# A two-layer hybrid block on one core: an instruction order planned with other durations, a fixed slack, the attention's second half ahead of a branch product, and 16-bit plane copies on ScalarE

## The chip, the cores and the metric

The kernel runs on 1 core of one Trainium2 chip. The metric is the device time of one execution in microseconds; lower is better. Engines are TensorE (PE; PEld is its weight load), VectorE (DVE), ScalarE (ACT), GpSimd (POOL) and SyncE (SP), which here issues nearly all DMAs.

## The reference

16 meta tokens and 256 input tokens (272 in all) of width 1024 go through two layers. A layer has a mixer of three branches and a feed-forward part:

```python
proj = rms_norm(h, g) @ w_in          # 12 parts: rq rk rv rg | hq hf hi hg | dq dk dv | mg
o_ret = retention(rq, rk, rv, rg)     # 4 heads, decayed causal attention, rms, * silu(gate)
o_hg  = hgrn2(hq, hf, hi, hg, lb)     # 8 heads, a gated recurrence with per-channel decay
o_da  = diff_attention(dq, dk, dv)    # 8 heads, softmax(.) - lam * softmax(.), times dv, rms
y = sum_n sigmoid(mg_n) * (branch_n @ w_branch[n])
h = h + y @ w_out
u = rms_norm(h, g2) @ w_ffn_in        # 5632 columns
c = conv_b + sum_j conv_w[j] * shift(u, j)      # 3 taps along tokens
h = h + (silu(gate half of c) * value half of c) @ w_ffn_out
```

A last rms_norm gives the output, 256 x 1024, in fp32.

## The kernel before, in words

Activations lie transposed: features on the 128 partitions, the 272 tokens along the free axis. The second layer computes 258 token columns where the earlier tokens' results are not needed (272 for keys, values and the recurrence's inputs).

**Large matmuls.** All weights come as one stream of 128 x 128 tiles, eight to a chunk of 512 KB. A chunk is fetched by SyncE (`wraw`, three buffers), ScalarE writes the rounded high part `whi`, VectorE the remainder `wlo` (four buffers each). The activations have high and low parts too (`xh` and `xl`, `b0hi` and `b0lo` and so on). A tile product is three matmuls, lines 915 to 917: `whi` by high, `whi` by low, `wlo` by high. Two column tiles of an output make a pair; a pair of a 1024-deep product is 16 tiles, 48 matmuls, and collects in one of two PSUM buffers named `main`. `products` issues it, `evacuate`, `rotate` (rotary embedding on VectorE) or a branch's own step reads it out.

**The list ORDER** names the pairs in the order in which TensorE takes them within a layer: `("b0", 2)` is the third pair of the first branch's product. Marks stand in between: `+name` traces the small work of a branch (`+hga`, `+hgb` the recurrence's two halves, `+hgoa`, `+hgob` their outputs, `+ret` retention, `+daa`, `+dab` the attention's two halves of four heads), `!name` sets the due time of that work, `*name` splits a branch's output into high and low parts. Small work means small fp32 matmuls on TensorE (tiles `lev`, `ho`, `ro`, `ds`, `wt`, `do`) linked to VectorE, ScalarE and GpSimd steps.

**The planner.** Nothing is issued while the program is traced. Every call becomes an operation with an engine, a cost in us (class `_Engine`), a key (the time on a clock made of the large matmuls' costs at which it is wanted), the tiles it touches, and what it depends on. `_Plan.order` then simulates the five engines: it takes again and again the operation that can start earliest, and among those that can start at the same moment the one with the lowest `rank`, mostly its key. A small matmul has its key plus HOLD (3.0), or minus PULL (8.0) where TensorE has just run another small matmul and its operands are SURE (0.3) old. BACK is charged for a return to large matmuls. A result is counted as seen by another engine CROSS (0.4) after its end. The order so found is written out; on the chip each engine takes its own queue in order and waits on semaphores. Costs are thus used to sort, never to delay.

`_Weights.next` gives a chunk's fetch and its two splits a key LEAD before the first tile's. `behind` traces a job of small work; within one kind a job's first operation is placed after the last operation of the job `apart` places before it. `settle` spreads the jobs' keys between the mark `+` and 12 us (MARGIN) before the mark `!`.

**Values.** v of each branch is needed with tokens on the partitions. `values` reads a pair out of PSUM into `vsrc` (ScalarE), and `to_tokens` turns it as 16-bit halves: two copies part the fp32 words into low and high planes (`apart`), SyncE issues two DMA transposes (`turned`), two more copies join the planes into `vt` or `rvt`. The copies were on GpSimd. There are 24 such pairs (hi, rv, dv: four each, in two layers). The three kinds of tile share four buffers.

GpSimd also does the sums over partitions for the norms of the heads (`hr`), small copies (`tails`, `dt`, `wts`), and eight multiplications by the row norm (`y`) where a norm is folded into the activations.

Of the kernel before, what the change touches and what calls it, by code (L numbers as in the profile page):

```python
# [39 lines left out]
SLOTS = 13  # L40
LEAD = 6.0
MARGIN = 12.0
# [5 lines left out]
HOLD, PULL = 3.0, 8.0  # L48
BACK = 0.09
SURE = 0.3  # L50


# [4 lines left out]
def _pairs(name, lo, hi):  # L57
# [18 lines left out]
    + [("+daa", 0), ("*b0", 0), ("!ret", 0), ("!hgob", 0)]  # L76
    + _pairs("dq", 2, 4) + _pairs("b0", 0, 4) + _pairs("dk", 2, 4) + _pairs("dv", 2, 4)
    + [("+dab", 0)]
    + _pairs("m1", 0, 4)
    + [("*b1", 0)]  # L80
# [276 lines left out]
class _Plan:  # L357
# [4 lines left out]
    FREE = 0.5  # L362
    SWITCH = 1.3
    SETS = {AF.Exp: "le", AF.Ln: "le", AF.Silu: "silu", AF.Sigmoid: "sigmoid"}

# [88 lines left out]
    def order(self):  # L454
# [15 lines left out]
        count = 0  # L470
        tables = "le"
        beside = False
# [22 lines left out]
        def rank(op, t):  # L495
            if op.engine == "pe" and op not in mains:
                return op.key - PULL if beside and op.fed + SURE <= t else op.key + HOLD
            late = 8.0 if op.func in self.SETS and self.SETS[op.func] != tables else 0.0
            return op.key + late
# [4 lines left out]
        while len(out) < todo:  # L504
# [69 lines left out]
class _Engine:  # L574
# [5 lines left out]
    def __getattr__(self, method):  # L580
        f = getattr(self.engine, method)

        def call(*args, **kw):
            aps = [(k, x) for k, x in list(enumerate(args)) + list(kw.items()) if isinstance(x, bass.AP)]
            outs = [x for k, x in aps if k in (0, "out", "accum_out")]
            ins = [x for k, x in aps if k not in (0, "out", "accum_out")]
            n = math.prod(outs[0].shape[1:])
            cost = self.fixed + self.each * n
            if self.name == "act":
                cost += 0.093 * (len(aps) - 2) - (0.043 if ins[0].tensor.name in self.plan.psum else 0.0)  # L590
            elif self.name == "pool" and method != "memset":
                cost += 1.6e-3 * n
            if method == "partition_all_reduce":
                cost = 0.4 + 5.4e-3 * n
            if method == "reciprocal":
                cost += 7 * self.each * n
            elif method == "tensor_tensor_scan":
                cost += self.each * n
            elif method == "transpose":
                cost = 0.11  # L600
            elif method == "matmul" and args[1].dtype == F32R:
                cost = max(0.107, n / 2400 + 0.003)
# [4 lines left out]
            self.plan.add(self.name, lambda: f(*args, **kw), cost, outs, ins, args[2] if method == "activation" else None)  # L607

        return call
# [57 lines left out]
def _trace(ctx, tc, plan, a, depth, probe):  # L667
    nc = tc.nc
    act = _Engine(plan, nc.scalar, "act", 0.094, 0.833e-3)
    dve = _Engine(plan, nc.vector, "dve", 0.068, 1.042e-3)  # L670
    pe = _Engine(plan, nc.tensor, "pe", 0.0, 4 / 2400)
# [220 lines left out]
    def products(xs, name, j, t0=0):  # L892
# [58 lines left out]
    def to_tokens(src, vt, e):  # L951
# [37 lines left out]
    for li in range(depth):  # L989
# [369 lines left out]

        def behind(f, until, apart=1):  # L1360


            plan.group = ops = []
            rest = f()
            plan.group = None
            plan.in_turn(ops)
            mine = chains.setdefault(until[:2], [])
            mine.append(ops)
            if len(mine) > apart:
                plan.queue(ops[0], mine[-1 - apart][-1])  # L1370
            jobs.append((until, clock[0], ops))
            return rest
# [24 lines left out]
        def final():  # L1397
# [15 lines left out]
            cost = 3 * (BANK / 2400 + 0.012)  # L1413
            groups = [(t, c) for t in range(2) for c in range(2)]
# [38 lines left out]
        for name, j in ORDER:  # L1453
# [9 lines left out]
            elif name in ("+daa", "+dab"):  # L1463
# [166 lines left out]
```

## Time and profile before

| | |
|---|---|
| median of 3 runs | 1304.77 us (1304.16 to 1307.01) |
| the profiled execution | 1305.7 us, span 1303.9 us |
| granted TensorE clock, mean | 0.998 |
| VectorE, ScalarE busy | 76%, 60% of the span |
| weight chunks fetched by SyncE | 402 of 512 KB and 4 of 256 KB |
| DMA transposes | 48, median 4.0 us from issue to landing |

The span runs from the first to the last instruction of the profiled execution; its time includes a little around it. In the profile, most of the program's instructions carry line 607 (before), where the helper that records every call issues them, so they are told apart by their tiles: `out<-in` after the engine and the operation. "Idle before, releaser" is the time in which an engine stood still before instructions of a group, and what ended most of it. A row of the windows view gives a stretch, then the busy time of PE, PEld, DVE, ACT and POOL in it with the count of instructions, the granted clock, the DMA engines' share and GB/s. A row of the waits view gives who waited for whom, the total in us, the number of times and the longest.

### The profile page before, as it was taken

What the parts mean: (1) busy time and instruction counts of PE and PEld (TensorE: products, weight loads), DVE (VectorE), ACT (ScalarE), POOL (GpSimd) and SP (SyncE); (2) the same over time, 40 slices, a digit from 0 to 9 for tenths busy, and PEclk for the clock granted to TensorE, in tenths of its full rate; (3) what the DMA queues carried; (4) which work ended last, traced back from release to release, by engine and by line L of the source; (5) the groups of instructions that cost most, each with busy time, mean ns of one, the idle gap of its engine ahead of it and who ended that gap; (6) DMA issues with size and microseconds to landing.
All of it is one profiled execution on the core that took longest, in us unless ns stands there. A gap on an engine that the chain in (4) does not pass through costs nothing.

```text
span 1303.9 us, 28637 instructions
## 1 busy us (share of the span) xinstructions
PE 1285.8 (99%) x11678; PEld 1256.7 (96%) x11678; DVE 986.7 (76%) x1589; ACT 786.7 (60%) x1282; POOL 270.3 (21%) x300
## 2 busy tenths in 40 slices
PE   9999999999999999999999999999999999999998
PEld 9999989999999999999999999899999999999986
DVE  7685897798686789886575768877986867898843
ACT  6746444746576567666456474447466765776643
POOL 5021262423422020000030212634223220200000
PEclk9999999999999999999999999999999999999999
DMA  7664665643744545555555646655446446466653
GB/s 272 200 179 147 173 178 155 164 160 125 199 138 157 182 156 178 183 173 183 175 178 185 186 149 185 179 155 168 159 138 199 145 162 198 144 207 196 201 190 112
DMA packets 86868, 225.36 MB, mean 173 GB/s; under 512 B 32976, under 2 KB 33104, under 8 KB 86736
## 3 DMA queue, kind: packets, MB, share of 16 engines
q1 hardware_dynamic: 86448, 223.00, 55.3%
q8 instruction: 92, 1.51, 0.5%
q10 hardware_dynamic: 288, 0.52, 0.1%
q14 instruction: 40, 0.33, 0.1%
HBM read 216.16 MB, written 1.05 MB: 167 GB/s over the span
## 4 chain that ended last, share of the span: by engine, by line
PE 88%; DVE 9%; issue 1%; ACT 1%; DMA 0%; SPq 0%; DVEq 0%; ACTq 0%
PE main L915 26%; PE main L917 26%; PE main L916 25%; DVE wlo L607 2%; PE fo L1430 2%; PE fo L1431 2%; PE fo L1429 2%; DVE two_b L607 1%; DVE two_a L607 1%; PE lev L1107 1%; PE ds L1291 1%; PE ho L607 1%; PE ro L607 1%; PE do L607 1%; DVE two_c L607 1%
## 5 line engine op out<-in xcount | busy, mean ns | idle before, releaser
L915 PE MATMUL main<-xh,whi 128*128 128x272 f32 (+1 forms) x2368 | 682.6, 288 | 0.8 <-ACT whi L607 0.8
L917 PE MATMUL main<-xh,wlo 128*128 128x272 f32 (+1 forms) x2368 | 673.9, 285 | 1.3 <-DVE wlo L607 0.7
L916 PE MATMUL main<-xl,whi 128*128 128x272 f32 (+1 forms) x2368 | 673.3, 284 | 1.5 <-DVE xl L607 1.5
L607 DVE TENSOR_TENSOR wlo<-wraw,whi 128x1024 fp32r<-128x1024 f32 (+1 forms) x411 | 512.0, 1250 | 187.8 <-ACT whi L607 186.6
L607 ACT ACTIVATE whi<-wraw 128x1024 fp32r<-128x1024 f32 (+1 forms) x411 | 427.5, 1042 | 250.9 <-PE main L916 166.3
L917 PEld LDWEIGHTS main<-xh,wlo 128*128 128x128 f32 x2368 | 446.5, 189 | 3.1 <-DVE wlo L607 2.3
L916 PEld LDWEIGHTS main<-xl,whi 128*128 128x128 f32 x2368 | 446.6, 189 | 2.2 <-DVE xl L607 1.9
L915 PEld LDWEIGHTS main<-xh,whi 128*128 128x128 f32 x2368 | 446.7, 189 | 2.0 <-ACT whi L607 1.0
L607 POOL TENSOR_TENSOR y<-h,rstd 128x272 f32<-128x272 f32 x32 | 34.6, 1112 | 318.1 <-ACT rstd L607 318.1
L607 POOL PARTITION_ALL_REDUCE hr<-hsq x36 | 65.8, 1837 | 88.9 <-ACT hsq L607 85.9
L607 DVE SCALAR_TENSOR_TENSOR two_b<-main,small,two_b 128x256 f32<-128x256 f32 (+2 forms) x144 | 65.3, 487 | 24.4 <-ACT two_b L607 22.7
L607 POOL COPY apart<-vsrc 128x512 uint16<-128x512 uint16 x48 | 40.7, 867 | 145.2 <-ACT vsrc L607 145.0
L607 ACT ACTIVATE two_b<-main,small 128x272 f32<-128x272 f32 (+1 forms) x72 | 37.3, 566 | 23.8 <-PE main L917 22.7
L915 PE MATMUL main<-ghi,whi 128*128 128x272 f32 x176 | 51.0, 290 | 0.0
L916 PE MATMUL main<-glo,whi 128*128 128x272 f32 x176 | 50.6, 287 | 0.0
L917 PE MATMUL main<-ghi,wlo 128*128 128x272 f32 x176 | 50.3, 286 | 0.0
L607 POOL COPY vt<-turned 128x512 uint16<-128x512 uint16 x32 | 37.0, 1160 | 29.2 <-DMA turned<-apart 29.0
L915 PE MATMUL main<-b0hi,whi 128*128 128x272 f32 (+1 forms) x128 | 37.9, 296 | 0.0
L915 PE MATMUL main<-b1hi,whi 128*128 128x272 f32 (+1 forms) x128 | 37.8, 296 | 0.0
L915 PE MATMUL main<-yhi,whi 128*128 128x272 f32 (+1 forms) x128 | 36.4, 284 | 0.0
L917 PE MATMUL main<-b0hi,wlo 128*128 128x272 f32 (+1 forms) x128 | 36.4, 284 | 0.0
L917 PE MATMUL main<-yhi,wlo 128*128 128x272 f32 (+1 forms) x128 | 36.3, 284 | 0.0
(235 smaller groups left out, 1970.1 us busy)
## 6 DMA issues: line engine op xcount, KB each, us to landing
wraw<-in_w SPq DMA_DIRECT2D x402, 512.0 KB, 3.4
h<-in_h SPq DMA_DIRECT2D x4, 272.0 KB, 5.1
dec<-in_dec SPq DMA_DIRECT2D x2, 544.0 KB, 4.9
wraw<-in_w SPq DMA_DIRECT2D x4, 256.0 KB, 4.2
const<-in_const SPq DMA_DIRECT2D x1, 937.0 KB, 5.6
turned<-apart SPq DMA_TRANSPOSE x48, 4.0
gain<-in_gl SPq DMA_DIRECT2D x1, 512.0 KB, 5.1
out<-y ACTq DMA_DIRECT2D x2, 256.0 KB, 2.8
```

Of the source, the lines that this page charges most:

```text
L607: self.plan.add(self.name, lambda: f(*args, **kw), cost, outs, ins, args[2] if method == "activation" else None)
L915: nc.tensor.matmul(o, wh, hi, start=first, stop=False)
L916: nc.tensor.matmul(o, wh, lo, start=False, stop=False)
L917: nc.tensor.matmul(o, wl, hi, start=False, stop=last)
L1107: nc.tensor.matmul(o, keys, x, start=True, stop=True)
L1291: nc.tensor.matmul(ss[m][:, at : at + nk], q[half, hd, q0 : q0 + P], k[half, hd, :nk], start=True, stop=True)
L1429: nc.tensor.matmul(o, gh, wh, start=False, stop=False)
L1430: nc.tensor.matmul(o, gl, wh, start=False, stop=False)
L1431: nc.tensor.matmul(o, gh, wl, start=False, stop=end)
```

## The change

Six things are changed; no operation is added or taken away.

- The costs that the planner gives to operations: fixed prices of ScalarE 0.094 to 0.2 and of VectorE 0.068 to 0.145 us, 0.01 instead of 0.003 us on each large matmul, own prices for GpSimd's copies, two-input operations and sums over partitions, 0.7 us more on a DMA transpose, and 8 us where GpSimd goes from two-input operations to sums over partitions or back.
- A small matmul whose operands are less than SAFE (1.0 us) old is ranked behind everything else. BACK becomes 0.
- LEAD goes from 6 to 8 us.
- In ORDER, the first branch's product b0 comes after dk and dv of the attention's second half and the mark `+dab`, not ahead of them.
- A head of the attention may start after the eighth operation from the end of the head two places before it, not after its last.
- The four plane copies of `to_tokens` are ScalarE activations (Copy), not GpSimd copies.

```diff
-LEAD = 6.0
+LEAD = 8.0
...
-BACK = 0.09
+BACK = 0.0
 SURE = 0.3
+SAFE = 1.0
...
-    + _pairs("dq", 2, 4) + _pairs("b0", 0, 4) + _pairs("dk", 2, 4) + _pairs("dv", 2, 4)
+    + _pairs("dq", 2, 4) + _pairs("dk", 2, 4) + _pairs("dv", 2, 4)
     + [("+dab", 0)]
-    + _pairs("m1", 0, 4)
+    + _pairs("b0", 0, 4) + _pairs("m1", 0, 4)
...
+    RELOAD = 8.0
...
             if op.engine == "pe" and op not in mains:
+                if op.fed + SAFE > t:
+                    return math.inf
                 return op.key - PULL if beside and op.fed + SURE <= t else op.key + HOLD
...
+            if e == "pool" and op.func is not None:
+                if op.func != code:
+                    code, t = op.func, max(t, engines[e] + self.RELOAD)
...
+            elif method == "tensor_scalar":
+                cost += 0.065 * (len(aps) - 2) - 0.14
+            elif method in ("scalar_tensor_tensor", "stream_shuffle", "tensor_tensor_reduce"):
+                cost += 0.06
...
+            elif self.name == "pool" and method == "tensor_tensor":
+                cost, kind = 0.55 + 2.1e-3 * n, method
+            elif self.name == "pool" and method == "tensor_copy":
+                cost = 0.5 + 1.6e-3 * n
+            elif method == "partition_all_reduce":
+                cost, kind = 0.2 + 6.3e-3 * n, method
...
-                cost = self.fixed + self.each * n * outs[0].shape[0]
+                cost = self.fixed + self.each * n * outs[0].shape[0] + (0.7 if kw.get("transpose") else 0.0)
...
-    act = _Engine(plan, nc.scalar, "act", 0.094, 0.833e-3)
-    dve = _Engine(plan, nc.vector, "dve", 0.068, 1.042e-3)
+    act = _Engine(plan, nc.scalar, "act", 0.2, 0.833e-3)
+    dve = _Engine(plan, nc.vector, "dve", 0.145, 1.052e-3)
...
-        cost = 3 * ((T - t0) / 2400 + 0.003)
+        cost = 3 * ((T - t0) / 2400 + 0.01)
...
-            pool.tensor_copy(apart[:, i].rearrange("p (c f x) -> p c f x", c=2, f=2),
-                             halves(src[:, :, : 2 * P], i).rearrange("p f (c x) -> p c f x", c=2))
+            act.activation(apart[:, i].rearrange("p (c f x) -> p c f x", c=2, f=2),
+                           halves(src[:, :, : 2 * P], i).rearrange("p f (c x) -> p c f x", c=2), AF.Copy)
...
-            pool.tensor_copy(halves(vt[:, :, e : e + 2 * P], i), turned[:, i].rearrange("p (c x) -> p c x", c=2))
+            act.activation(halves(vt[:, :, e : e + 2 * P], i), turned[:, i].rearrange("p (c x) -> p c x", c=2), AF.Copy)
...
-        def behind(f, until, apart=1):
+        def behind(f, until, apart=1, after=1):
...
-            mine.append(ops)
+            mine.append((ops, after))
             if len(mine) > apart:
-                plan.queue(ops[0], mine[-1 - apart][-1])
+                before, which = mine[-1 - apart]
+                plan.queue(ops[0], before[-which])
...
-                    behind(lambda: da_head(b, hd), "da", 2)
+                    behind(lambda: da_head(b, hd), "da", 2, 8)
```

More of the change, by code (lines that the diff above doesn't have):

```diff
@@ L470, in order @@
         count = 0
-        tables = "le"
+        tables, code = "le", "tensor_tensor"
         beside = False
@@ L588, in call @@
             cost = self.fixed + self.each * n
+            kind = args[2] if method == "activation" else None
             if self.name == "act":
                 cost += 0.093 * (len(aps) - 2) - (0.043 if ins[0].tensor.name in self.plan.psum else 0.0)
[L591 to L595, printed above, removed]
-                cost += 7 * self.each * n
-            elif method == "tensor_tensor_scan":
-                cost += self.each * n
+            elif method == "tensor_scalar":
+                cost += 0.065 * (len(aps) - 2) - 0.14
+            elif method in ("scalar_tensor_tensor", "stream_shuffle", "tensor_tensor_reduce"):
+                cost += 0.06
+            elif method == "reciprocal":
+                cost += 7 * self.each * n
+            elif self.name == "pool" and method == "tensor_tensor":
[4 more added lines that the diff above has]
+                cost, kind = 0.2 + 6.3e-3 * n, method
             elif method == "transpose":
                 cost = 0.11
-            elif method == "matmul" and args[1].dtype == F32R:
-                cost = max(0.107, n / 2400 + 0.003)
             elif method == "matmul":
@@ L605, in call @@
             elif method == "dma_start":
-                cost = self.fixed + self.each * n * outs[0].shape[0]
-            self.plan.add(self.name, lambda: f(*args, **kw), cost, outs, ins, args[2] if method == "activation" else None)
+                cost = self.fixed + self.each * n * outs[0].shape[0] + (0.7 if kw.get("transpose") else 0.0)
+            self.plan.add(self.name, lambda: f(*args, **kw), cost, outs, ins, kind)
         return call
@@ L1412, in final @@
                     pe.matmul(accs[t][k // 4][:, k % 4 * P : (k % 4 + 1) * P], h[:, k, tokens(t)], ident, is_transpose=True, start=k % 4 == 0, stop=False)
-            cost = 3 * (BANK / 2400 + 0.012)
+            cost = 3 * (BANK / 2400 + 0.0133)
             groups = [(t, c) for t in range(2) for c in range(2)]
```

## The prediction

> **What bounds the kernel now.** I read the page's busy table first, then TensorE's own waits, then the stages in which those waits lie, then what GpSimd does there.
>
> ```profile
> span 1303.9 us, 28637 instructions
> ## 1 busy us (share of the span) xinstructions
> PE 1285.8 (99%) x11678; PEld 1256.7 (96%) x11678; DVE 986.7 (76%) x1589; ACT 786.7 (60%) x1282; POOL 270.3 (21%) x300
> ```
>
> TensorE is busy for 1285.8 of 1303.9 us, and the change removes no matmul. So what can be won by order alone is TensorE's idle time, 18.1 us at most, and whatever its instructions lose inside their busy time. The list of who TensorE waited for, longest first, says where the idle time is:
>
> ```profile
> PE lev L1107 <- DVE hf L607: 3.2, 2, 1.7
> PE main L916 <- DVE xl L607: 1.5, 2, 1.1
> PE ho L607 <- DVE ho L607: 1.4, 2, 0.8
> PE wt L1317 <- DVE two_a L607: 1.1, 3, 0.5
> PE warm L607 <- POOL eps L607: 1.0, 1, 1.0
> PE main L915 <- ACT whi L607: 0.8, 1, 0.8
> PE main L917 <- DVE wlo L607: 0.7, 3, 0.3
> PE lev L1107 <- DVE tot L607: 0.4, 1, 0.4
> PE lev L1107 <- DVE hq L607: 0.4, 1, 0.4
> PE main L917 <- issue: 0.4, 1, 0.4
> PE do L607 <- DVE tw L607: 0.4, 1, 0.4
> ```
>
> These eleven rows hold 11.3 us (total, times, longest). Two kinds stand in it. Small matmuls of the chains (lev of the HGRN2 levels, ho of its outputs, wt and do of the attention) were put into TensorE's queue before VectorE had their operands: 3.2 + 0.4 + 0.4 = 4.0 us for lev, 1.4 + 1.1 + 0.4 = 2.9 us for ho, wt and do. And the large ones waited at the start and at the feed-forward's first tiles, 1.5 + 1.0 + 0.8 + 0.7 + 0.4 = 4.4 us. VectorE ends nearly all of it. So I looked at the two stages with lev of the second half (155 to 206 and 806 to 860 us), at the stages of dv's first half, and at the stretch after the longest wait:
>
> ```profile
> 155.00:206.00 51.00, 48.83 (x761) 47.34 (x760) 45.28 (x70) 25.44 (x44) 31.19 (x33) 1.00 0.77 187
> 243.00:266.00 23.00, 22.19 (x181) 22.01 (x180) 18.22 (x21) 15.92 (x26) 16.12 (x17) 1.00 0.64 161
> 806.00:860.00 54.00, 51.86 (x781) 50.44 (x779) 45.53 (x70) 25.58 (x44) 32.30 (x34) 0.97 0.71 178
> 895.00:920.00 25.00, 24.43 (x199) 24.23 (x198) 19.59 (x27) 16.70 (x28) 16.09 (x17) 1.00 0.59 166
> ...
> 834.00:836.00 2.00, 2.00 (x10) 2.00 (x10) 2.00 (x4) 1.43 (x3) 0.06 (x1) 0.50 0.52 135
> 836.00:838.00 2.00, 2.00 (x65) 1.85 (x67) 0.59 (x1) 0.00 (x0) 0.00 (x0) 0.71 0.79 211
> ```
>
> The columns are PE, PEld, DVE, ACT, POOL busy, then granted clock. Three things are to be seen. In the lev stage VectorE works 45.28 of 51 us and ScalarE only 25.44, so the engine that ends the waits is nearly full, and another is half empty. GpSimd, elsewhere at 21% of the span, works 31.19 us there. And in the second layer TensorE's clock falls: 0.50 from 834 to 836 and 0.71 from 836 to 838, which is 2 x 0.50 + 2 x 0.29 = 1.6 us of full-speed work lost right after lev's 1.7 us wait.
>
> **The 16-bit planes.** The groups of the stage 155 to 206 us show why VectorE is slow there:
>
> ```profile
> L607 DVE TENSOR_TENSOR wlo<-wraw,whi 128x1024 fp32r<-128x1024 f32 x14 | 19.1, 1370 | 3.0 <-ACT whi L607 2.8
> L607 ACT ACTIVATE whi<-wraw 128x1024 fp32r<-128x1024 f32 x14 | 14.8, 1056 | 7.3 <-PE main L916 6.3 <-ACT at L607 1.0
> L607 POOL COPY apart<-vsrc 128x512 uint16<-128x512 uint16 x12 | 9.8, 839 | 20.7 <-ACT vsrc L607 20.6
> L607 POOL COPY rvt<-turned 128x512 uint16<-128x512 uint16 x8 | 7.2, 924 | 12.6 <-DMA turned<-apart 12.6
> L607 POOL COPY vt<-turned 128x512 uint16<-128x512 uint16 x4 | 5.4, 1340 | 2.4 <-DMA turned<-apart 2.2
> ...
> L607 ACT ACTIVATE vsrc<-main 128x544 f32<-128x544 f32 x6 | 3.7, 623 | 4.7 <-PE main L917 4.5 <-issue 0.3
> ```
>
> wlo takes 1370 ns on average in this stage; its median over the whole run, by the view of that tile, is 1224:
>
> ```profile
> L607 DVE TENSOR_TENSOR wlo<-wraw,whi x411: 418/1224/2232, 6.0 to 1288.0; 128x1024 fp32r<-128x1024 f32 x132, 128x512 fp32r<-128x512 f32 x4, 128x256 fp32r<-128x256 f32 x1
> ```
>
> That is 12% more while GpSimd copies. If the rest of VectorE's work there is stretched alike, 45.28 x (1 - 1224/1370) = 4.8 us of the 45.28 come back when the copies leave GpSimd; I take that as the upper end, for some of GpSimd's work stays, and 0 as the lower.
>
> The copies now cost ScalarE. No row shows it on 16-bit elements. The nearest is vsrc, 544 elements in 623 ns, so 512 cost about 0.62 us; the far end is GpSimd's own time:
>
> ```profile
> L607 POOL COPY apart<-vsrc 128x512 uint16<-128x512 uint16 x48 | 40.7, 867 | 145.2 <-ACT vsrc L607 145.0
> L607 POOL COPY vt<-turned 128x512 uint16<-128x512 uint16 x32 | 37.0, 1160 | 29.2 <-DMA turned<-apart 29.0
> ...
> L607 POOL COPY rvt<-turned 128x512 uint16<-128x512 uint16 x16 | 15.7, 1011 | 27.7 <-DMA turned<-apart 27.7
> ```
>
> So 48 + 32 + 16 = 96 copies move; GpSimd loses 40.7 + 37.0 + 15.7 = 93.4 us and ScalarE gains 96 x 0.62 = 60 (93 at the far end). I take 0.62, since whi, also ScalarE's, keeps 1056 ns in the very stage where wlo is stretched. In 155 to 206 us ScalarE goes from 25.44 to 25.44 + 24 x 0.62 = 40.3 of 51; in 243 to 266 from 15.92 to 20.9 of 23. On its average it fits. What is new is the wait: a joining copy waits for its transposing DMA, and what stands behind it in ScalarE's queue is whi of the weights to come, then wlo on VectorE, then the large matmuls. The cover is this row of the waits over all engines:
>
> ```profile
> ACT whi L607 <- PE main L916: 166.3, 134, 2.9
> ```
>
> 134 times ScalarE stood ready and waited for a whi buffer, so mostly it is ahead by all four. I charge 0.7 us for the planes, with 0 and 12.2 (worked out under the rivals) as ends.
>
> **The true durations and the slack.** The planner priced a large tile at 3 x (272/2400 + 0.003) = 0.349 us, and a chunk's wlo at 0.068 + 1024 x 0.001042 = 1.135 us. Before, wlo took 1.224, and VectorE's shorter instructions, which carry the larger fixed price now, were under-priced by more. So small matmuls were queued for a moment at which VectorE was not ready. That is the first kind of wait: 4.0 us of lev, 2.9 of the others, and the 1.6 us of clock. With the true prices and 1.0 us of slack (SAFE) a small matmul is ranked behind the large ones until its operands are 1 us old in the plan. What hides that delay are large matmuls, which are nearly always ready. What is late next is then the chain itself, and its jobs are spread over tens of microseconds. I let 80% of it go, as VectorE stays near full in the lev stage: (4.0 + 1.6) x 0.8 = 4.5 and 2.9 x 0.8 = 2.3 us.
>
> [...]
>
> The price of the slack is that runs of small matmuls may break into more pieces. Each return to large ones costs something inside TensorE's busy time:
>
> ```profile
> 135.09 0.38 PE L915 MATMUL main<-xh,whi 128*128 128x272 f32 x1
> 135.31 0.29 PE L916 MATMUL main<-xl,whi 128*128 128x272 f32 x1
> 135.44 0.28 PE L917 MATMUL main<-xh,wlo 128*128 128x272 f32 x1
> ```
>
> From the timeline of TensorE, just after an ho run: the first large matmul holds the next back by 0.22 us, the second by 0.13. A return costs 0.09. BACK leaves the plan, but nothing on the chip changes by that. Between 10 returns fewer and 16 more (one for each of the 2 x 8 attention heads) the end is -0.9 to +1.5; I take +0.5.
>
> **LEAD of 8.** Weights are fetched and split 2 us earlier in the plan. At the feed-forward's first tiles (xl, wlo: 1.5 + 0.7) this helps; I take 0.8 of the 4.4 us of the second kind, bounds 0 and 2.2. At the very start it moves the second chunk's DMA ahead of the second pair of h tiles: its key goes from 3 - 6 = -3 to 3 - 8 = -5, and that pair has 1.4 x 2 - 7 = -4.2. The first 30 us move
>
> ```profile
> DMA packets 3025, 8.49 MB, mean 283 GB/s; under 512 B 464, under 2 KB 592, under 8 KB 3024
> ```
>
> so 512 KB in front of those tiles cost 0 to 1.85 us; I take 0.7, as both are needed by the same matmuls.
>
> **The second half first.** b0's four pairs (DMA stream, 192 large matmuls, four VectorE products) go behind dk and dv of the second half, so its attention may begin four pairs, about 24 us, earlier (48 matmuls of 0.125 us a pair), and b0's operand slots are held that much longer. The heads have more room up to the same due time; wt and do above are what this can save, so I charge it with nothing further, between -1 and +1.5 us (their waits gone, or as much again). The DMA's 0.7 us, the 8 us that the plan now charges GpSimd for a change of its code and the other prices act only through order: nothing more.
>
> Sum: -4.5 - 2.3 - 0.8 + 0.7 + 0.5 + 0.7 = -5.7 us. The profiled execution took 1305.7 us (span 1303.9); that gives 1300.0. The median of the three runs, 1304.77, lies 0.9 below the profiled one, so the forecast is 1299.1 us. With every term at its kind end (-5.6, -2.9, -2.2, 0, -0.9, 0 and -1 for the order) it is 1292.2; with -4.5, -2.3, 0, +1.85, +1.5 and +0.7 it is 1302.
>
> **Rivals.** *ScalarE's queue stalls behind the transposes (slower).* In the rows above GpSimd waited 12.6 + 2.2 = 14.8 us for them in 155 to 206 us, 29.0 + 27.7 = 56.7 in all. If ScalarE sits through the same, it needs 40.3 + 14.8 = 55.1 of 51 us, 4.1 too many, and the like in the second layer; with 56.7/48 = 1.2 us for each of four joins, 243 to 266 needs 20.9 + 4.7 = 25.6 of 23, and 895 to 920 16.7 + 5.0 + 4.7 = 26.4 of 25. Together 4.1 x 2 + 2.6 + 1.4 = 12.2 us. It decides once a join waits over (51 - 40.3)/12 = 0.9 us on average in the first stage. With this price whole, and the other terms (-6.4) kept, the profiled sum is 1311.5 and the time 1310.6. For it: the transposes share SyncE's queue with the weights. Against: GpSimd had nothing better to do while it waited, and 134 waits for whi buffers are cover. Chance 0.24.
>
> *The waits only move (no change).* VectorE's 45.28 of 51 us stay a deficit, since it gets back little of the 4.8; a small matmul that comes later is then still too early, or its chain pushes a later one. With half of 4.5 + 2.3 gone and the start, returns and planes at their worse middles (1.0 + 1.0 + 1.0), the sum is -3.4 - 0.4 + 3.0 = -0.8: 1304.0. Chance 0.13.
>
> *The clock drops all the same.* If the half-clock stretch hangs on something other than the wait, or returns at another gap, 1.3 of the 4.5 us stay: 1300.4. Chance 0.06. [...]
>
> **How the numbers follow.** The forecast has 0.57, and its own range is 1292 to 1302. About 0.2% (2.6 us) is what a measurement of this kernel can tell from no change. Faster: 0.57 + 0.06, less 0.01 that ends within the bound, 0.62; same 0.14; slower 0.24. The range that leaves out no more than 2 in 10 runs from the kind end, 1292, to just above the slower rival, 1311.
>
> **What the changed profile would show.** Right: lev's waits for VectorE under 1 us in sum, no window under clock 0.9 near 830 us, wlo near 1.25 us in the values' stages, POOL near 177 us busy and ACT near 847, the 96 copies near 0.62 us. Wrong: ScalarE's joining copies waiting for the transposes by more than 0.9 us each with main matmuls waiting for whi or wlo behind them; copies near 1 us; a second-layer clock still at 0.50; or main waiting at 6 to 14 us for xl of the h tiles by over 1 us more.

## The result, and the profile after

| | before | after |
|---|---|---|
| median beside each other | 1305.67 us | 1301.59 us |
| ratio, with its 95% interval | | 0.9977 [0.9968, 0.9986] |
| the profiled execution | 1305.7 us, span 1303.9 | 1303.02 us, span 1301.2 |

The change makes the kernel faster by 0.23%, 3.0 us (1.8 to 4.2). The forecast was 5.7 us: the sign is right and the size about half. The busy table of the changed kernel answers to the one of before:

```profile
span 1301.2 us, 28596 instructions
## 1 busy us (share of the span) xinstructions
PE 1285.1 (99%) x11678; PEld 1257.0 (97%) x11678; DVE 960.2 (74%) x1589; ACT 831.8 (64%) x1374; POOL 167.7 (13%) x204
```

The copies moved as they should: GpSimd has 102.6 us less, ScalarE 45.1 more, and VectorE, which has the same 1589 instructions, works 26.5 us less. (ScalarE's groups by themselves add up to 58.9 us more, 896.7 against 837.8; time in which two of its instructions overlap in the trace counts once in the busy table.) TensorE's own waits in the changed kernel, the whole list (total, times, longest):

```profile
PE main L926 <- DVE xl L617: 5.8, 6, 1.9
PE main L927 <- DVE wlo L617: 2.0, 4, 0.7
PE warm L617 <- POOL eps L617: 1.0, 1, 1.0
PE main L925 <- DVE dq L617: 0.8, 1, 0.8
PE main L925 <- DVE dk L617: 0.2, 1, 0.2
PE main L925 <- ACT xh L617: 0.2, 1, 0.2
```

Every wait of a small matmul is gone: 4.0 us of lev and 2.9 of ho, wt and do. In their place stand waits of the large ones: for xl 5.8 instead of 1.5 us, for wlo 2.0 instead of 0.7, for the rotation of dq (it holds the PSUM buffer) 0.8. The windows of the stages shown before, and of a stretch that is new (PE, PEld, DVE, ACT, POOL, then granted clock):

```profile
155.00:206.00 51.00, 51.00 (x773) 49.69 (x775) 38.85 (x65) 38.76 (x68) 5.17 (x9) 1.00 0.84 198
243.00:266.00 23.00, 23.00 (x186) 22.84 (x185) 15.33 (x25) 20.99 (x32) 4.46 (x9) 1.00 0.55 161
806.00:860.00 54.00, 54.00 (x813) 52.73 (x812) 42.92 (x72) 39.80 (x71) 4.41 (x10) 1.00 0.81 198
895.00:920.00 25.00, 25.00 (x205) 24.89 (x204) 20.92 (x37) 20.80 (x37) 10.56 (x11) 1.00 0.53 167
...
834.00:836.00 2.00, 2.00 (x75) 1.83 (x74) 0.58 (x2) 1.46 (x2) 0.21 (x1) 1.00 0.41 80
...
1131.00:1133.00 2.00, 1.23 (x5) 1.23 (x6) 2.00 (x6) 2.00 (x5) 0.00 (x0) 0.66 0.57 217
1133.00:1135.00 2.00, 2.00 (x11) 2.00 (x11) 2.00 (x4) 0.48 (x2) 0.00 (x0) 0.50 0.00 0
```

TensorE is now busy in all of the four stages, VectorE has fallen from 45.28 to 38.85 us in the first, and the clock at 834 us is full. It is 0.66 and 0.50 at 1131 to 1135 instead: 2 x 0.34 + 2 x 0.50 = 1.7 us lost there.

Where the time came from and went is read from TensorE's timeline, by the start of the first large matmul of a pair (us; the pair's place follows from ORDER and 48 matmuls a pair):

```
                                           before +   after, copies   after, old   last kernel
first matmul of           before   after   copies     on GpSimd       prices       below
layer 1  hf 3              37.6     42.1     37.6        40.3           38.9         37.2
         rv 0             161.4    165.2    161.4       163.4          162.1        160.4
         dq 0             193.0    192.8    191.1       192.3          189.9        187.9
         first ffn pair   466.9    466.9    464.9       465.0          463.8        461.2
layer 2  rv 0             814.2    814.6    812.3       813.5          811.5        808.6
         dq 0             847.1    842.2    840.0       840.2          839.0        835.3
         first ffn pair  1110.1   1105.6   1103.6      1106.4         1102.2       1100.5
span                     1303.9   1301.2   1297.4      1300.8         1296.6       1295.6
```

The changed kernel loses 4.5 us before hf 3, wins 4.0 and 5.3 us in the two lev stages (rv 0 to dq 0), and gives 1.8 back after 1110. Elsewhere it differs by under 1 us. Both half clocks are in these numbers: about 1.7 of the 5.3 us is the one that the profiled execution of before had at 834, and the 1.8 us after 1110 are nearly all the one at 1131.

### The profile page after: what moved, and what is told of

Same layout as the page of the kernel before. It is cut to its first block, busy times and chain, and to the rows that moved or that the text cites. A ratio compares the mean times of both kernels' runs of the same rounds, so it can differ in the third digit from the quotient of the medians.

```text
span 1301.2 us, 28596 instructions
## 1 busy us (share of the span) xinstructions
PE 1285.1 (99%) x11678; PEld 1257.0 (97%) x11678; DVE 960.2 (74%) x1589; ACT 831.8 (64%) x1374; POOL 167.7 (13%) x204
## 4 chain that ended last, share of the span: by engine, by line
PE 92%; DVE 6%; issue 1%; DMA 1%; ACT 0%; SPq 0%; DVEq 0%
PE main L925 27%; PE main L926 27%; PE main L927 27%; DVE wlo L617 2%; PE fo L1442 2%; PE fo L1441 2%; PE fo L1440 2%; PE lev L1117 1%; DVE two_b L617 1%; PE ds L1301 1%; PE ro L617 1%; PE do L617 1%; DMA wraw<-in_w 1%; PE ho L617 1%; DVE xl L617 1%
## 5 line engine op out<-in xcount | busy, mean ns | idle before, releaser
L617 DVE TENSOR_TENSOR wlo<-wraw,whi 128x1024 fp32r<-128x1024 f32 (+1 forms) x411 | 505.1, 1236 | 179.3 <-ACT whi L617 178.6
L617 POOL PARTITION_ALL_REDUCE hr<-hsq x36 | 74.2, 2077 | 128.1 <-ACT hsq L617 127.9
L617 ACT ACTIVATE two_b<-main,small 128x272 f32<-128x272 f32 (+1 forms) x72 | 37.7, 566 | 26.7 <-PE main L927 26.7
L617 ACT ACTIVATE m<-main 128x544 f32<-128x544 f32 (+1 forms) x24 | 14.7, 614 | 39.5 <-PE main L927 39.5
L927 PE MATMUL main<-b1hi,wlo 128*128 128x272 f32 (+1 forms) x128 | 36.5, 285 | 0.5 <-DVE wlo L617 0.5
L926 PE MATMUL main<-b1lo,whi 128*128 128x272 f32 (+1 forms) x128 | 36.4, 284 | 0.0
```

What stands on the lines that cost most here:

```text
L926: nc.tensor.matmul(o, wh, lo, start=False, stop=False)
L927: nc.tensor.matmul(o, wl, hi, start=False, stop=last)
```

## The experiments

The gain in us is (1 - ratio) x 1305. The interval is the ratio's, at 95%.

| kernel | ratio | interval | gain, us |
|---|---|---|---|
| the change | 0.9977 | 0.9968 - 0.9986 | 3.0 |
| before + copies on ScalarE | 0.9961 | 0.9946 - 0.9975 | 5.1 |
| the same, ScalarE's price nudged | 0.9964 | 0.9951 - 0.9978 | 4.7 |
| the same, VectorE's price nudged | 0.9955 | 0.9941 - 0.9968 | 5.9 |
| before + copies + slack | 0.9969 | 0.9956 - 0.9981 | 4.0 |
| before + copies + all new prices | 1.0050 | 1.0038 - 1.0063 | -6.5 |
| ... only ScalarE's and VectorE's | 1.0018 | 1.0009 - 1.0028 | -2.3 |
| ... only the large matmuls' | 0.9986 | 0.9977 - 0.9994 | 1.8 |
| ... only GpSimd's, with the 8 us | 1.0015 | 1.0006 - 1.0025 | -2.0 |
| ... only GpSimd's, without them | 0.9984 | 0.9974 - 0.9993 | 2.1 |
| before + LEAD 8 | 1.0023 | 1.0014 - 1.0032 | -3.0 |
| the change, copies on GpSimd | 0.9987 | 0.9978 - 0.9995 | 1.7 |
| the change, no slack | 1.0017 | 1.0008 - 1.0026 | -2.2 |
| the change, LEAD 6 | 0.9996 | 0.9987 - 1.0005 | 0.5 |
| the change, b0 first again | 0.9992 | 0.9983 - 1.0002 | 1.0 |
| the change, old prices | 0.9953 | 0.9941 - 0.9965 | 6.1 |
| the change, h fetched first | 0.9978 | 0.9969 - 0.9987 | 2.9 |
| the change, start repaired | 0.9967 | 0.9956 - 0.9979 | 4.3 |
| the last kernel below | 0.9941 | 0.9928 - 0.9953 | 7.7 |

My first theory was that the change is what I had forecast, less a start that was put in disorder. The rival: the planner's part is worth little or less than nothing, and the copies carry the gain.

**The copies alone.** Before, with the copies on ScalarE and nothing else:

```diff
-            pool.tensor_copy(apart[:, i]...
+            act.activation(apart[:, i]..., AF.Copy)
...
-            pool.tensor_copy(halves(vt...
+            act.activation(halves(vt..., AF.Copy)
```

> The kernel before with the plane copies on ScalarE alone, old prices and order rules. If the copies' going frees VectorE where lev waits (forecast): wlo near 1.22 us in 155 to 206 us, lev's waits fall from 4.0 us, time 1302 to 1304. If what counts is the plan's prices and slack: within 1 us of 1305.7 or slower, with lev, ho and wt still waiting about 7 us. If ScalarE's queue stalls behind the transposes: slower by over 3 us, with main waiting for whi or wlo.

It gains 5.1 us, more than the 1302 to 1304 us expected of it and, by the middle values, more than the whole change (the intervals overlap in a small part). Its list of TensorE's waits, whole:

```profile
PE main L916 <- DVE xl L607: 1.5, 2, 1.2
PE wt L607 <- DVE wts L607: 1.5, 2, 1.1
PE wt L1317 <- DVE two_a L607: 1.3, 3, 0.5
PE warm L607 <- POOL eps L607: 1.0, 1, 1.0
PE main L917 <- DVE wlo L607: 0.5, 2, 0.3
PE lev L1107 <- issue: 0.4, 1, 0.4
```

lev no longer waits for VectorE and neither does ho, with the old prices and no slack; the attention's wt does, and the start is as it was (hf 3 at 37.6). Its windows of the lev stages:

```profile
155.00:206.00 51.00, 50.57 (x777) 49.17 (x776) 40.97 (x72) 40.21 (x69) 5.57 (x9) 1.00 0.77 197
806.00:860.00 54.00, 54.00 (x810) 52.62 (x809) 42.78 (x78) 41.36 (x72) 6.36 (x10) 1.00 0.74 192
```

VectorE is busy 4.3 us less in the first, close to the 4.8 that I had worked out and left out of the sum, and over the whole run 25.6 us less with the same 1589 instructions (986.7 to 961.1).

**LEAD of 8 on the kernel before** (`LEAD = 6.0` to `8.0`):

> The kernel before with LEAD 8 alone. T1: 4 us slower at the start, as the fetch order there becomes that of the changed kernel, up to 1 us won back elsewhere: 1308 to 1310. T2: no change, 1305 to 1306. T3: slower by the two feed-forward starts, about 2 us, 1307 to 1308, with the start unchanged.

3.0 us slower. The fourth fetch of h goes out at 8.18 instead of 4.96 us, hf 3 begins at 39.4 instead of 37.6, and the large matmuls wait 4.1 us for xl. So LEAD 8 does harm at the start by itself, 1.8 us; the other 1.2 us are lost later.

**LEAD of 6 in the changed kernel** (`LEAD = 8.0` to `6.0`):

> The changed kernel with LEAD back at 6. Theory T1 (the loss sits in SyncE's queue at the start: with LEAD 8 the fourth chunk's fetch, which waits for a wraw buffer, stands ahead of the last pair of h tiles): the fourth h fetch is issued near 5 us instead of 8.55, rstd is ready near 21.5 us instead of 26.3, the pair hf 3 starts near 37.6 us instead of 42.1, and the time falls by about 4.5 us, to 1297. Rival T2 (true durations, not LEAD, delay the folded activations on GpSimd and VectorE): the start stays as in the changed kernel and the time stays within 1 us of 1301.6. T3 (LEAD 8 costs mostly at the two feed-forward starts, by putting wlo ahead of xl on VectorE): the waits of 1.5 us near 492 and 2.2 us near 1129 us go, the start stays, 1298.

It loses 2.5 us against the change, though h is fetched as before: the start stays late (hf 3 at 42.3), and the large matmuls wait 3.9 us for wlo, eight times. My first theory expected 1297 us and is refuted: LEAD is not what holds up the start of the changed kernel. With the new prices the longer lead pays; in the kernel before it does not.

**The start.** First the fetches of h moved ahead, then also the squares of the norm, and the slack kept away from the first norm's matmul:

```diff
 # both
-plan.key = -9.0 if k == 0 else 1.4 * k - 7.0
+plan.key = -9.0 if k == 0 else 1.4 * k - 9.0
 # the second alone
-                plan.key = 1.0 + 2.5 * j
+                plan.key = -1.5 + 2.5 * j
...
-                if op.fed + SAFE > t:
+                if op.key > 30.0 and op.fed + SAFE > t:
```

> The changed kernel with LEAD 8 kept and the keys of the h fetches put 2 us earlier, so that SyncE issues them in the order of the kernel before; nearly all the rest of the order stays. T1: the start as in the kernel before (hf 3 near 37.6 us), 4 to 4.5 us less, 1297 to 1297.6. T2 and T3: no change, 1301 to 1302.

> The changed kernel with three things at the start alone: the h fetches' keys 2 us earlier (as in e2_h_first), the four squares of the first norm 2.5 us earlier, and no slack for the first norm's matmul. T4 (the start lost 4.5 us to late rstd, by three causes in one chain: SyncE's order, the squares behind whi on ScalarE, and the slack on the norm's matmul): rstd done near 21.5 us, hf 3 near 37.6 to 38 us, time 1297 to 1298. T5 (the start's loss is given back before the end, since later waits absorb it): the start improves and the time stays at 1301 to 1302.

The first moves hf 3 from 42.1 to 40.7 and nothing in the time (0.9978): at rv 0 of the second layer it stands at 814.6 us, as the changed kernel does, after a new wait of 1.0 us for two_b. The second brings hf 3 to 38.4. The time shows 1.3 of those 3.7 us, within the intervals; in the profiled execution 2.7 are left at the second layer's first feed-forward pair (1102.9 against 1105.6), behind a wait of 0.8 us for two_b. So the start's loss is real, but what is won there is partly waited away later.

**Slack** (`SAFE = 1.0` to `-99.0` in the changed kernel), **and the slack alone on before with the copies:**

> The changed kernel without the slack: a small matmul may be taken as soon as the plan has its operands. If the slack is what took away lev's, ho's and wt's waits: they come back, 5 to 7 us, less 2 us at the start: 1304 to 1307. If the copies' move did that alone: these waits stay under 2 us, the start gains up to 2 us: 1299 to 1301.

> The kernel before with the plane copies on ScalarE and the slack of 1 us, old prices and all else. Compare with e5_before_planes_act (1299.6). If the slack takes away e5's waits of wt for VectorE (2.8 us) and costs 2 us at the first norm's matmul: 1298 to 1300 with hf 3 near 39 us. If it takes away nothing: 1301 to 1302.

Without it the changed kernel is slower by 5.2 us, with new waits of wt for dm and dt (1.1 us each), 3.2 for wlo, and a start that is 2.1 us better (hf 3 at 40.0). The waits of lev and ho for VectorE, which I had expected back, stay away. On the old prices the slack does nothing that the intervals separate (0.9969 against 0.9961): wt's waits go, but the third branch's product waits 3.3 us for b2hi and b2lo. So the slack is worth something beside the new prices, and nothing that shows beside the old ones; why, these runs do not say.

**The order** (b0 ahead of dk and dv again, in the changed kernel):

> The changed kernel with b0 again ahead of dk and dv of the second half. If the new ORDER is what gives the attention time to end before the third branch product: main waits for b2hi or b2lo by 2 to 4 us, as in e12_planes_slack, and the waits for dq and dk near 287 us (1.0 us) go: 1303 to 1305. If the new ORDER only bunches the rotations: 1300 to 1301.

2.0 us slower by the middle values; the intervals overlap a little. Waits for b2hi (0.8 us) and b2lo (0.9) are there, less than the 2 to 4 us expected; they are gone where the second half comes first. The earlier start of the heads and BACK 0 were not undone by themselves.

**The copies back on GpSimd** in the changed kernel:

> The changed kernel with the plane copies on GpSimd, all else kept. If the copies are where the gain came from: lev's stages (rv 0 to dq 0) take 4 to 5 us more in each layer or their waits come back, 1306 to 1308. If the prices and the slack were enough: within 2 us of 1301.6.

VectorE's time goes back to 981.7 us, lev waits 1.2 us for it and ho 1.0. The loss is 1.3 us, which the intervals do not separate, so this is the outcome written down for "the prices and the slack were enough", not the 1306 to 1308 us of the other. The table of positions agrees: without the copies' move the lev stages take 28.9 and 26.7 us, 8.9 less than before; the copies alone save 7.1 there, the whole change 9.3. Either of the two takes most of the same waits away, so they overlap and do not add.

**The prices.** The changed kernel with the old prices, then before with the copies and the new prices (the diff of the change, cut to its prices):

> The changed kernel with the old prices; LEAD 8, slack, new ORDER, earlier heads and ScalarE's copies stay. T6 (the new prices cost time: at the start they put the squares behind whi): rstd near 23 us (LEAD's part stays), hf 3 near 39.5 us instead of 42.1, time 1297 to 1299. Rival T7 (the prices pay for themselves later, through fewer early small matmuls): the start gains 2 to 3 us, lev, ho and wt wait 3 us and more again, 1301 to 1303.

> The kernel before with the plane copies on ScalarE and the new prices, without LEAD 8, slack, new ORDER, earlier heads or BACK 0. Compare with e5_before_planes_act (1299.6), which has the old prices. If the new prices put the squares behind whi at the start: rstd near 23 us instead of 20.9, hf 3 near 39 to 40 us instead of 37.6, 1301 to 1303. If the prices help (forecast): lev, ho and wt wait less than e5's 2.8 us, 1297 to 1299.

Within the change the new prices cost 3.1 us, alone 11.6 (1.0050 against 0.9961). The 3.1 us lie at the start: with the old prices hf 3 begins at 38.9 instead of 42.1 us, and at every later pair in the table the kernel is ahead by 2.9 to 3.4. TensorE's list for the second, its first four rows:

```profile
PE main L927 <- DVE wlo L617: 5.6, 9, 1.6
PE main L926 <- DVE xl L617: 3.4, 3, 1.2
PE main L925 <- ACT b2hi L617: 1.8, 1, 1.8
PE lev L1117 <- issue: 1.7, 2, 1.2
```

The large matmuls, which were to hide the small ones' delay, wait themselves: 5.6 us for wlo where before it was 0.7. hf 3 begins at 42.0, with h fetched as before: the late start comes with the prices. The lev stages gain by them, 26.7 and 26.7 us against 29.7 and 27.7 with the copies alone. From dq 0 to the first feed-forward pair, where the attention lies, the kernel takes 4.2 and 9.0 us more, 1.7 of the 9.0 at half clock. Which prices? One group at a time on before with the copies:

```diff
 # e15: ScalarE's and VectorE's: 0.094 -> 0.2, 0.068 -> 0.145, and by operation
 # e16: large matmuls: 3 * ((T - t0) / 2400 + 0.003) -> ... + 0.01
 # e17: GpSimd's and RELOAD = 8.0;  e18: the same with RELOAD = 0.0
```

> Before with the copies on ScalarE and only the new prices of ScalarE's and VectorE's instructions. Before with the copies alone had the ratio 0.9961, with the copies and all new prices 1.0050: 11.8 us lie between. Theory F (the splits' prices do it: with 0.2 and 0.145 us of fixed price ScalarE and VectorE look fuller in the plan, so ScalarE's order at the start changes and the splits of the weights come later): 1.003 to 1.005, rstd done at 25 us or later, waits of main for wlo of 4 us or more. Theory M (the large matmuls' price does it): 0.996 +- 0.001, rstd done near 21.5. Theory G (GpSimd's prices and its 8 us do it): as under M.

> Before with the copies on ScalarE and only the new price of the large matmuls (0.01 instead of 0.003 us on each, 0.0133 instead of 0.012 in the last product). Theory M (the plan's clock is stretched by 6%, so all other work looks faster against it and is issued later): 1.003 to 1.005, waits of main for wlo of 4 us or more. Theory F or G: 0.996 +- 0.001. If the old and the new prices only differ in how they fall together: each of these runs 0.996 to 0.999 and no one reaches 1.003.

> Before with the copies on ScalarE and only GpSimd's new prices with the 8 us for each change of its code. Theory G (GpSimd's work looks 8 us late wherever it alternates, and what hangs on it is placed late): 1.002 or more, with waits of main for xl, b2hi and b2lo. Theory F or M: 0.996 +- 0.001.

> As the run with GpSimd's new prices, but with 0 in place of the 8 us. If the 8 us matter, it is 0.002 or more below that run (0.996 +- 0.001); if not, the two agree within 0.001.

Each group loses against the copies alone by its middle value: 7.4, 3.3 and 7.0 us, of the last 4.0 by the 8 us. (The interval of GpSimd's prices without the 8 us just touches that of the copies alone.) No theory of one culprit holds. The three together would be 17.7 and are 11.6. ScalarE's and VectorE's prices bring the waits for wlo (4.6 us, six times) and 2.0 of the late start, GpSimd's 5.2 for xl and 1.2 of the start, and the large matmuls' price neither: its hf 3 begins at 37.2, but lev's waits come back (3.0 us).

So is any other plan some us worse, and the copies' 5.1 us a lucky one? Two nudges that make no price truer:

```diff
-    act = _Engine(plan, nc.scalar, "act", 0.094, 0.833e-3)
+    act = _Engine(plan, nc.scalar, "act", 0.098, 0.833e-3)
 # the other kernel: dve, 0.068 -> 0.071
```

> Before with the copies on ScalarE, and ScalarE's fixed price 0.098 instead of 0.094 us: a change that makes no price truer. It only gives the list scheduler other ties to break. Theory S (each group of prices harms by what it says): the ratio stays at that of the copies alone, 0.9961 +- 0.001. Theory L (any other order is some us away, and 0.9961 is a lucky one): 0.998 or more.

> The same with VectorE's fixed price 0.071 instead of 0.068 us. Theory S: 0.9961 +- 0.001. Theory L: 0.998 or more, and the two nudged kernels differ by 0.001 or more from each other.

Both stay where the copies alone are (0.9964, 0.9955), although 133 and 162 of the 1589 places in VectorE's queue hold another instruction. The copies' gain is no luck, and plans that far apart differ by under 1 us. GpSimd's prices without the 8 us change about as many places (199) and lose 3.0 us, which the intervals just fail to separate. ScalarE's and VectorE's prices change 846, so for them the yardstick says less: what chance does in so different a plan was not tried.

**The version the experiments point to:** the copies, the new ORDER, the attention's earlier start and BACK 0, with the old prices, LEAD 6, and the slack for all but the first norm.

```diff
-LEAD = 8.0
+LEAD = 6.0
...
-                if op.fed + SAFE > t:
+                if op.key > 30.0 and op.fed + SAFE > t:
 # and all prices as in the kernel before
```

> Old prices, LEAD 6, ScalarE's copies, the slack for every small matmul but the first norm's, the new ORDER, earlier heads, BACK 0. T6: the start as in the kernel before (hf 3 near 37.6 us), no waits of lev, ho, wt, no wait for b2hi, 1295 to 1297. T7: 1299 to 1301, not under e5_before_planes_act.

Its median is 1297.41 us, 0.9941 of before: faster than both kernels. From the copies alone (0.9961) and from the change with the old prices (0.9953) the intervals do not separate it. Its two longest waits of TensorE:

```profile
PE main L924 <- DVE xl L615: 2.3, 2, 1.9
PE vm L615 <- POOL tails L615: 1.1, 1, 1.1
```

## Why the prediction was right or wrong, step by step

**The step that failed.** The sum had the start at +0.7 us, and the start cost 4.5. These 3.8 us are more than the 2.7 by which the result missed the forecast. Behind them stands a cost that the prediction put at nothing without a reason: that of the new prices. Those of ScalarE and VectorE were counted for the waits that they were to remove, and the others "act only through order: nothing more". In the changed kernel they cost 3.1 us, and in the profiled executions the whole distance is there at hf 3. The waits of the small matmuls, in the sum at -6.8 us, are not where the forecast fell short: the lev stages alone gained 9.3 us, 1.7 of it clock. The planes' term was wrong as well, but to the other side: with its sign right the forecast would have been further from the result.

**The planes on ScalarE (+0.7, bounds 0 and 12.2): wrong in sign.** The size of a copy was right for one half and short for the other; the groups of ScalarE, whole run, and what it waited for:

```profile
L617 ACT ACTIVATE apart<-vsrc 128x512 uint16<-128x512 uint16 x48 | 27.9, 620 | 0.0
L617 ACT ACTIVATE vt<-turned 128x512 uint16<-128x512 uint16 x32 | 24.8, 786 | 1.5 <-DMA turned<-apart 1.5
...
L617 ACT ACTIVATE rvt<-turned 128x512 uint16<-128x512 uint16 x16 | 12.2, 782 | 3.9 <-DMA turned<-apart 3.8
```

27.9 + 24.8 + 12.2 = 64.9 us stand against the 60 forecast: the joining copies, which write every second 16-bit element, take 0.78 and not 0.62 us. The cover held: ScalarE sat 5.3 us behind transposes in the whole run, where the slower rival needed 56.7, and no large matmul waits for whi. What I left out was the other side. I had worked out that VectorE gets up to 4.8 of its 45.28 us back, and then named that only an upper end and put nothing of it into the sum. It got back 4.3 with the copies alone and 6.4 with the whole change (from the windows above; the last holds five of its instructions fewer). The copies alone take away the waits of lev and ho for VectorE and gain 5.1 us. Both bounds lay at 0 or above; a gain was excluded without a reason.

Where the gain comes from is in the groups of the first lev stage, the first row with the copies alone, then two of the changed kernel:

```profile
L607 DVE TENSOR_TENSOR wlo<-wraw,whi 128x1024 fp32r<-128x1024 f32 x14 | 17.1, 1233 | 3.9 <-ACT whi L607 3.9
...
L617 DVE TENSOR_TENSOR wlo<-wraw,whi 128x1024 fp32r<-128x1024 f32 x16 | 19.3, 1221 | 6.9 <-ACT whi L617 6.9
L617 ACT ACTIVATE whi<-wraw 128x1024 fp32r<-128x1024 f32 x15 | 15.8, 1052 | 5.2 <-PE main L926 4.5 <-DMA wraw<-in_w 0.6
```

wlo is at 1233 and 1221 ns where it was 1370; in the second lev stage the step is smaller, 1280 before and 1226 after. whi on ScalarE is as before, 1052 against 1056. A comparison inside the trace of the kernel before leaves the plan out of it: the 292 wlo of 1024 elements during which no GpSimd instruction ran took 1221 ns on average, the other 107 took 1396; whi took 1057 (286 of them) and 1056 ns (113). With the copies alone, 64 wlo instead of 107 have GpSimd beside them. How this becomes a wait of lev is in VectorE's timeline before, in the two steps that make the operands of the lev that waits 1.70 us, until 832.5:

```profile
829.40 1.24 DVE L607 TENSOR_TENSOR hq<-hq,tot 128x544 f32<-128x544 f32 x1
...
831.26 1.09 DVE L607 TENSOR_TENSOR hf<-hf,tot 128x544 f32<-128x544 f32 x1
```

With the copies alone the same two steps take 0.72 and 0.76 us. A rival is left: GpSimd's own remaining work was quicker too (the copies `tails` 10.5 instead of 20.9 us). That the waits named VectorE speaks against it; no run tells the two apart. Nor does one show why wlo takes longer beside GpSimd: the rows only have wlo lose 175 ns on average there, and whi nothing.

**True durations and slack (-4.5 and -2.3): right on the waits, wrong in counting no cost.** All of the waits and the half clock at 834 went, and the lev stages gained 9.3 us against 6.8 forecast for all such waits. With the copies back on GpSimd they still gain 8.9, with 2.2 us of waits left, so prices, slack and order are enough for it; the copies alone give 7.1. Prices and slack were not run apart without the copies. But the prices called true (a wlo has 1.222 us by the new one, 1.135 by the old, 1.221 in the trace with no GpSimd instruction beside it) cost 3.1 us within the change and 11.6 beside the copies alone. The step assumed that a plan with truer costs is a better one, and that the large matmuls are nearly always ready to hide a delay. One of its own rows was against it: ScalarE's 134 waits for a whi buffer, 166.3 us, said that the large matmuls were well fed under the old prices. In the changed kernel, with LEAD 8 even, that cover is smaller:

```profile
ACT whi L617 <- PE main L926: 138.5, 119, 2.8
```

How a truer price leads to a later wlo the runs do not show.

**LEAD of 8 at the start (+0.7, bounds 0 and 1.85): too low, and not the main cause.** The start cost 4.5 us. TensorE's busy time in the first 42 us, first of before, then of after:

```profile
0.00:42.00 42.00, 39.82 (x300) 38.82 (x301) 31.64 (x37) 30.61 (x44) 17.84 (x22) 1.00 0.74 252
```

```profile
0.00:42.00 42.00, 37.29 (x264) 35.20 (x265) 31.67 (x36) 28.72 (x42) 17.32 (x22) 1.00 0.72 245
```

36 matmuls fewer are done by then, 36 x 0.125 = 4.5 us. I had costed the transfer of 512 KB. SyncE's queue shows what was missed, in before and then in after:

```profile
4.96 0.48 SPq L607 DMA_DIRECT2D h<-in_h  x1
```

```profile
8.18 0.33 SPq L617 DMA_DIRECT2D wraw<-in_w  x1
8.55 0.43 SPq L617 DMA_DIRECT2D h<-in_h  x1
```

The weights' fetch ahead of h has to wait for one of the three wraw buffers (it goes out 0.03 us after a wlo has ended, at 8.15), and the last quarter of h stands 3.6 us behind it. That is one part, 1.8 us by the kernel with LEAD 8 alone. Two more come in: with the new prices the last square of the first norm stands behind two whi on ScalarE (at 18.35 instead of 15.85 us), and the slack ranks the norm's matmul ms behind large ones (24.6 instead of 19.8). By the runs above hf 3 begins 3.2 us earlier without the new prices, 2.1 without the slack, and no earlier with LEAD 6: the parts overlap. In the timelines of ScalarE, before and after:

```profile
20.42 0.49 ACT L607 ACTIVATE rstd<-ms,eps 128x272 f32<-128x272 f32 x1 [1.97 <-PE ms L607]
```

```profile
25.31 0.49 ACT L617 ACTIVATE rstd<-ms,eps 128x272 f32<-128x272 f32 x1 [1.44 <-PE ms L617]
```

rstd is 4.9 us late, so are y, xh and xl of the folded norm, and the large matmuls wait for xl, 2.6 us in these 42 against none before. Most of it is at 36.87 and 40.59 us in TensorE's timeline, not at 6 to 14 as I had put it:

```profile
36.87 0.39 PE L926 MATMUL main<-xl,whi 128*128 128x272 f32 x1 [0.73 <-DVE xl L617]
...
40.59 0.39 PE L926 MATMUL main<-xl,whi 128*128 128x272 f32 x1 [1.21 <-DVE xl L617]
```

**LEAD of 8 at the feed-forward (-0.8, bounds 0 and -2.2): wrong in sign.** At the feed-forward's first pairs the waits for xl rose from 1.5 to 3.2 us. LEAD has a part in it: alone, in the kernel before, it raises them to 2.5, and LEAD 6 in the changed kernel lowers them to 2.1. It is not all, for the last kernel, with LEAD 6, waits 1.92 us at the second of these places. In VectorE's queue of the changed kernel, xl stands there behind a wlo, a glo and four steps of the convolution, 3.1 us in all. TensorE's timeline:

```profile
1129.50 0.39 PE L925 MATMUL main<-xh,whi 128*128 128x258 f32 x1 [0.16 <-ACT xh L617]
1131.77 0.58 PE L926 MATMUL main<-xl,whi 128*128 128x258 f32 x1 [1.88 <-DVE xl L617]
1132.15 0.42 PE L927 MATMUL main<-xh,wlo 128*128 128x258 f32 x1
1132.37 0.42 PE L925 MATMUL main<-xh,whi 128*128 128x258 f32 x1
```

1.88 us of waiting, and behind it matmuls 0.22 us apart instead of 0.12, until 1135.1.

**Order (0, bounds -1 and +1.5).** It is worth 2.0 us in the changed kernel, by waits for b2 and not for wt and do. That is beyond -1 by its middle value, but the intervals do not settle it. **Returns (+0.5)** could not be told apart from the rest.

**Rivals.** The slower one is refuted by the 5.3 us above. The waits moved in part, from small matmuls to xl and wlo, as the second rival says; its reason (VectorE still full) is wrong, for VectorE is at 38.85 of 51. The third came true at another place: the clock dropped all the same, at 1131. That the time came within 2.7 us of the forecast owes something to luck: a gain that was left out and a loss that was left out stood against each other.

## What to carry to other kernels

Cost a move to another engine on both sides: what the receiving engine pays, and what the engine that worked beside the old one gets back; here the copies alone were worth 5.1 us, and the sum had them as a loss. A planner's prices, lead and slack act on each other: each is to be tried alone, truer prices too, with a nudge that means nothing as a yardstick for what chance does. Two changes that each remove the same wait are to be counted once. And a fetch that is moved ahead in a queue can cost more than its transfer: here it waited for its buffer, and what stood behind it waited too.

## What of the hardware was not expected

TensorE's clock went to 0.50 after a wait of 1.9 us that ended at 1131.8 us, as it had at 834 after 1.7 before; both times matmuls were 0.21 to 0.23 us apart for some 3.4 us (from 833.8 to 837.2 and from 1131.8 to 1135.1). The last kernel has a wait of 1.92 us for xl at the same place, and its clock stayed full (PE, PEld, DVE, ACT, POOL, clock):

```profile
1126.00:1128.00 2.00, 0.57 (x5) 0.37 (x4) 1.96 (x5) 1.46 (x3) 0.00 (x0) 1.00 0.14 55
1128.00:1130.00 2.00, 1.50 (x12) 1.51 (x13) 2.00 (x7) 1.37 (x2) 0.00 (x0) 1.00 0.61 170
```

Seven more of the kernels above wait 1.88 to 2.02 us at this place, and none of their profiled executions lost clock there (the mean clock of the whole run is 0.999 in five of them and 0.997 in two); one that waits 2.16 us did (0.998). The kernel with copies and slack lost it at 422 us, behind two waits of 0.67 and 0.93 us (the granted clock is 0.86 from 418 to 430). So a wait of 1.9 us can bring the drop and need not, and shorter ones can. It also differs between executions of one kernel: those of the kernel before have mean clocks from 0.997 to 1.000, and one such drop takes 0.0013 of the span. What decides is not settled here.
